# Column totals of an attention kernel moved into the idle PSUM bank of the attention's outputs

## The chip, the cores and the metric

The kernel runs on one core of a Trainium2 chip. The metric is device time in microseconds of one execution. A core has TensorE (PE, with weight loads shown apart as PEld), VectorE (DVE), ScalarE (ACT), GpSimd (POOL) and SyncE (SP, which here issues nearly all DMAs). Matmuls write to PSUM; this kernel cuts PSUM into eight banks of 512 fp32 columns by 128 partitions. A matmul that begins a new use of a bank must wait until the engines that read the bank's last content are done.

## The reference, cut to what matters

One layer of a streaming encoder: 2048 prompt rows and 8 streams of 16 rows with 512 cached keys. Rows are normed, modulated and projected; two attentions run side by side; their outputs are gated, projected, merged and projected again.

```python
qa, ka, va, za, qb, kb, vb, zb, ga, gb = project_inputs(h, w_in[l], pos_p)
oa = diff_attention(qa, ka, va, qpos, kpos, lam)          # A: softmax(q1 k1) - lam softmax(q2 k2), 4 heads
ob = stick_breaking_attention(qb, kb, vb, qpos, kpos)     # B: sigmoids and a running product, 8 heads
ya = (rms_norm(oa, subln_g) * (1 - lam_init) * silu(za)) @ w_branch_a
yb = (ob * silu(zb)) @ w_branch_b
x = x + gate * ((sigmoid(ga) * ya + sigmoid(gb) * yb) @ w_out)
```

All is fp32 outside. The kernel multiplies in fp16, with each operand cut into a high and a low half. For that it needs a power of two as scale of each weight piece and cache piece, and it gets one from the sum of squares of the whole piece: ACT sums the squares along each partition, and a matmul with a 128x128 matrix of ones adds the 128 partition sums up and hands the total to all partitions.

## The kernel before, in words

The attention's work is cut into eight units, `u` = 0 to 7: unit 2h is head h of A, unit 2h+1 is two heads of B. Each unit has 17 row tiles of 128 rows: the sample tile first (`NT`), then prompt tiles t = 0 to 15. A step is one tile of one unit:

- `project` (L467): 24 matmuls of 128x512 into a bank of tag "mm"; ACT and DVE cut the result into fp16 halves of q, k and v. In units of B, `gate_piece` (L543) adds 24 more matmuls per tile, which sum up in the bank of tag "t", and ACT (L548) takes them out.
- `transpose_qk` (L561, L565): six transposes into the bank "t", which DVE or ACT copies out (L575, L576).
- `scores`: for each 512 keys two matmuls (L708, L709) and, at the diagonal, a mask (L712), into a bank of tag "s". For A DVE takes the scores out (L602) and a softmax follows. For B ACT writes two sigmoids (L134), DVE scans them (L682), and POOL multiplies (L688).
- `turn`: the weights are cut into halves (L616, L619; for A L318, L323) and a transposing DMA on SP (L626) brings them into a buffer `wt`, of which there are five (8 blocks of 128 keys each).
- `pv`: the weights times the values, block by block: for A three matmuls (L765 to L767), for B two for each of two heads (L769, L770). They sum up in a bank of tag "o" from the tile's first block to its last, 3(t+1) matmuls for A and 4(t+1) for B. ACT (L744, L749) and DVE (L750) then take the tile out. These products are put off by 27 time units of the kernel's own count, some one and a half tiles.

The PSUM banks before: two of "mm", three of "s", one of "t", two of "o", each tag used in turn. The column totals of `total` (L235, two instructions of a 128x1 product in fp32) went to these:

- `bounds` (L368, in `prepare_unit`): the total of the weights of unit u+1, into "t". DVE computes the scale from it (L243) and copies it (L371). Eight times in the run.
- `bounds_g` (L374): the same for the gate weights of a unit of B, into "t". Four times.
- `halve` (L951): the total of a piece of the cached keys, into "s". DVE reads it (L951), and the piece is then cut into halves on POOL and DVE. 32 times, spread over units 1 to 6.

`kernel` opens the tile framework with `schedule_with_timeline_sim=True`: the framework takes the instructions in the order in which the Python code makes them as their priority, and writes each engine's stream in the order in which, by its own model, operands and buffers come free. So the order of the instructions on an engine is not that of the code, and a tag with fewer buffers or another tag for a tile can move many instructions. Buffers of one tag are handed out in the order of the code. On the chip each engine runs its stream strictly in order.

Of the kernel before, what the change touches and what calls it, by code (L numbers as in the profile page):

```python
# [17 lines left out]
F32 = mybir.dt.float32  # L18
# [4 lines left out]
ALU = mybir.AluOpType  # L23
# [5 lines left out]
KT = D // P  # L29
# [95 lines left out]
def layer_kernel(ctx: ExitStack, tc: tile.TileContext, a: dict):  # L125
    nc = tc.nc
    V, S, G, T = nc.vector, nc.scalar, nc.gpsimd, nc.tensor
# [68 lines left out]
    unit = ctx.enter_context(tc.tile_pool(name="unit", bufs=2))  # L196
# [9 lines left out]
    kvp = c01.enter_context(tc.tile_pool(name="kvp", bufs=2))  # L206
    stg = c01.enter_context(tc.tile_pool(name="stg", bufs=2))

    BANKS = {"mm": 2, "s": 3, "t": 1, "o": 2}

    def bank(tag, dt=F32):
        return ps.tile([P, 512 if dt == F32 else 1024], dt, tag=tag, name=f"ps_{tag}", bufs=BANKS[tag])


# [17 lines left out]
    def total(col, n=1, tag="t"):  # L232

        p = bank(tag)
        T.matmul(p[:, 0:n], ones, col, start=True, stop=True)  # L235
        return p[:, 0:n]
# [66 lines left out]
    def add_up(acc, n):  # L303
        if n == 1:
            return acc[:, 0:1]
        col = tiny.tile([P, 1], F32, tag="col", name="col")
        V.tensor_reduce(out=col, in_=acc[:, 0:n], axis=AX.X, op=ALU.add)
        return col
# [26 lines left out]
    def prepare_unit(u, keep=None):  # L335
# [3 lines left out]
        U = dict(h=h, kind=kind, u=u, w=[], wg=[], bufs=[])  # L339
# [3 lines left out]
        gk = 1024 // gw if gw else 0  # L343
# [21 lines left out]
            return [lambda i=i: piece(i) for i in range(len(ks) + 2)]  # L365

        def bounds():
            fsq = total(add_up(U["wacc"], 4))  # L368
            U["sw"] = scales(fsq, unit, "sw")
            U["fsq"] = unit.tile([P, 1], F32, tag="fsq", name="fsq")  # L370
            V.tensor_copy(out=U["fsq"], in_=fsq)  # L371

        def bounds_g():
            U["sg"] = scales(total(add_up(U["gacc"], KT // gk)), unit, "sg")  # L374

        def split_to(name, k):

# [428 lines left out]
    def cache_column(name, h):  # L806
        return "ab".index(name[0]) * 4 + h
# [106 lines left out]
    def norms():  # L914
# [32 lines left out]
        def halve():  # L947
            st, name, h, i, acc = squared.pop(0)
            c = tiny.tile([P, 3], I32, tag="csc", name="csc", bufs=2)
            f = cexp[:, cache_column(name, h), i : i + 1]  # L950
            V.tensor_scalar(out=c[:, 0:1].bitcast(F32), in0=total(acc, 1, "s"), scalar1=2.0 ** -46, scalar2=None, op0=ALU.max)  # L951
            V.tensor_scalar(out=f, in0=c[:, 0:1], scalar1=24, scalar2=None, op0=ALU.logical_shift_right)
            V.tensor_scalar(out=c[:, 1:2], in0=f, scalar1=-1.0, scalar2=204.0, op0=ALU.mult, op1=ALU.add)
            V.tensor_scalar(out=c[:, 2:3], in0=c[:, 1:2], scalar1=23, scalar2=None, op0=ALU.logical_shift_left)
            to = free.pop(0)
            w = P // 2
            x = to.bitcast(F16).rearrange("p (j f n) -> p j f n", f=2, n=w)
            split(x[:, :, 0, :], x[:, :, 1, :], st.rearrange("p (j n) -> p j n", n=w), c[:, 2:3].bitcast(F32), G)
            load(out=keys_d[name, h, i], in_=x.rearrange("p (j c) f d -> p j (c f d)", c=1))
            free.append(st)  # L960
            free.append(to)
# [3 lines left out]
        def stages(k):  # L965
            if k > 1:
                halve()
            if 0 < k <= len(todo):
                square()
            if k < len(todo):  # L970
                fetch(*todo[k])
# [82 lines left out]
    with tc.tile_pool(name="p0", bufs=1) as p0:  # L1054
# [128 lines left out]
        def wide(x):  # L1183
# [24 lines left out]
                        scalar1=sh[:, 0:1], scalar2=None, op0=ALU.mult)  # L1208
# [208 lines left out]
    for n in range(len(steps) + 2):  # L1417
        made, qk, side = [], [], []
        if n < len(steps):
            u, t = steps[n]  # L1420
# [215 lines left out]
```

## Time and profile before

| what | value |
|---|---|
| runs before | 2221.84, 2226.48, 2226.58 us, median 2226.48 |
| the profiled execution | 2225.32 us, of which the span of the instructions is 2223.5 us |
| PE busy | 2061.2 us (93%) |
| DVE, ACT, POOL busy | 1743.8 (78%), 1606.2 (72%), 699.6 us (31%) |
| mean granted TensorE clock | 0.980 |

In the trace the run has three stages: up to some 136 us the modulation and the norms, up to some 1755 us the eight units, then the branch and output projections with the sample's attention. Busy times of PE are modelled from pipelined matmuls. In the lists of waits a row names the instruction that waited, the one that released it, the sum in us, how often, and the longest.

### The profile page before, as it was taken

What the parts mean: (1) busy time and instruction counts of PE and PEld (TensorE: products, weight loads), DVE (VectorE), ACT (ScalarE), POOL (GpSimd) and SP (SyncE); (2) the same over time, 40 slices, a digit from 0 to 9 for tenths busy, and PEclk for the clock granted to TensorE, in tenths of its full rate; (3) what the DMA queues carried; (4) which work ended last, traced back from release to release, by engine and by line L of the source; (5) the groups of instructions that cost most, each with busy time, mean ns of one, the idle gap of its engine ahead of it and who ended that gap; (6) DMA issues with size and microseconds to landing.
All of it is one profiled execution on the core that took longest, in us unless ns stands there. A gap on an engine that the chain in (4) does not pass through costs nothing. (4 is left out here: it accounts for less than half of the span.)

```text
span 2223.5 us, 41495 instructions
## 1 busy us (share of the span) xinstructions
PE 2061.2 (93%) x14608; PEld 1110.4 (50%) x14608; DVE 1743.8 (78%) x3799; ACT 1606.2 (72%) x3212; POOL 699.6 (31%) x608
## 2 busy tenths in 40 slices
PE   5999999999999999999999998989998788899997
PEld 3655555555555455555554554555454444444443
DVE  4667869789887788988778888777789877787864
ACT  3978677789877677978677788876688666666531
POOL 1232014356410443742024355301334412111210
PEclk8999999999999999999999999999999899999999
DMA  9778559899796889979879999985787999999762
GB/s 323 258 241 201 120 139 217 181 227 203 200 252 158 222 201 202 207 205 221 198 195 216 191 224 207 241 181 130 159 170 155 201 280 255 230 254 224 194 166 67
DMA packets 824978, 451.05 MB, mean 203 GB/s; under 512 B 556122, under 2 KB 763274, under 8 KB 824256
## 3 DMA queue, kind: packets, MB, share of 16 engines
q1 hardware_dynamic: 823820, 448.01, 82.7%
q8 instruction: 114, 1.87, 0.3%
q14 instruction: 96, 0.79, 0.1%
q10 hardware_dynamic: 948, 0.39, 0.1%
HBM read 229.87 MB, written 86.02 MB: 142 GB/s over the span
## 5 line engine op out<-in xcount | busy, mean ns | idle before, releaser
L688 POOL TENSOR_TENSOR sc_p<-sc_p,sc_n 128x127 f32<-128x127 f32 (+7 forms) x192 | 313.3, 1635 | 663.1 <-DVE sc_n L682 510.6
L467 PEld LDWEIGHTS <-hs 128*128 128x128 f16 x3120 | 293.3, 99 | 318.5 <-issue 6.4
L467 PE MATMUL ps_mm<-wa,hs 128*128 128x512 f16 x1590 | 391.2, 382 | 5.3 <-DMA hs<-hT_d 5.0
L467 PE MATMUL ps_mm<-wb,hs 128*128 128x512 f16 x1530 | 377.4, 380 | 0.0
L682 DVE TENSOR_TENSOR_SCAN sc_n<-ps_s,sc_n,zero_t 128x512 f32<-128x512 f32 x192 | 245.4, 1278 | 33.3 <-ACT ps_s L134 28.1
L708 PE MATMUL ps_s<-k,qst 128*128 128x512 f16 (+3 forms) x640 | 223.2, 350 | 30.0 <-DVE sc_n L682 22.8
L543 PEld LDWEIGHTS <-hs 128*128 128x128 f16 x1632 | 155.0, 98 | 181.7 <-DVE qst L576 5.1
L543 PE MATMUL ps_t<-wa,hs 128*128 128x512 f16 x1020 | 242.3, 380 | 2.1 <-DVE qst L576 2.0
L619 DVE TENSOR_TENSOR sc_n<-sc_p,sc_n 128x128 f16<-128x128 f32 (+7 forms) x192 | 217.7, 1137 | 32.9 <-ACT sc_n L616 32.3
L134 ACT ACTIVATE sc_p<-ps_s,usc 128x512 f32<-128x512 f32 (+3 forms) x320 | 203.9, 637 | 34.4 <-PE ps_s L709 23.0
L709 PE MATMUL ps_s<-k,qst 128*128 128x512 f16 (+3 forms) x640 | 223.6, 350 | 0.0
L616 ACT CAST sc_n<-sc_p 128x128 f16<-128x128 f32 (+7 forms) x192 | 155.0, 809 | 57.3 <-POOL sc_p L688 55.8
L134 ACT ACTIVATE ps_s<-ps_s,usc 128x512 f32<-128x512 f32 (+3 forms) x320 | 196.3, 613 | 0.0
L543 PE MATMUL ps_t<-wb,hs 128*128 128x512 f16 x612 | 151.7, 383 | 4.8 <-DMA hs<-hT_d 2.1
L769 PE MATMUL ps_o<-v,wt 128*128 128x128 f16 x1088 | 135.2, 224 | 22.1 <-DMA wt<-sc_n 21.9
L1535 PE MATMUL ps_o<-wo,wb 128*128 128x512 f16 x624 | 141.6, 382 | 1.1 <-ACT wb L1309 1.1
L602 DVE TENSOR_SCALAR_CACHE_REDUCE sc_p<-ps_s,usc 128x512 f32<-128x512 f32 (+3 forms) x160 | 106.2, 664 | 35.7 <-PE ps_s L709 20.5
L770 PE MATMUL ps_o<-v,wt 128*128 128x64 f16 x1088 | 127.1, 196 | 0.0
L769 PEld LDWEIGHTS <-wt 128*128 128x128 f16 x1088 | 101.0, 100 | 50.1 <-DMA wt<-sc_n 25.3
L682 DVE TENSOR_TENSOR_SCAN sc_n<-ps_s,zero_t 128x128 f32<-128x128 f32 (+3 forms) x128 | 104.0, 813 | 27.7 <-ACT ps_s L134 27.7
L1501 PEld LDWEIGHTS <-wa 128*128 128x128 f16 x816 | 77.7, 98 | 94.2 <-issue 4.1
L1544 POOL TENSOR_TENSOR x<-m,x 128x512 f32<-128x512 f32 x32 | 45.6, 1427 | 247.1 <-DVE m L1539 138.7
(378 smaller groups left out, 4548.6 us busy)
## 6 DMA issues: line engine op xcount, KB each, us to landing
hs<-hT_d SPq DMA_DIRECT2D x132, 512.0 KB
g_d<-gt SPq DMA_DIRECT2D x68, 256.0 KB
out_dram<-pr SPq DMA_DIRECT2D x204, 64.0 KB
o_d<-o SPq DMA_DIRECT2D x136, 64.0 KB
wa<-g_d SPq DMA_DIRECT2D x17, 512.0 KB
wb<-g_d SPq DMA_DIRECT2D x17, 512.0 KB
hs<-o_d SPq DMA_DIRECT2D x17, 512.0 KB
wide<-in_w_ada_dram SPq DMA_DIRECT2D x8, 1024.0 KB
```

Of the source, the lines that this page charges most:

```text
L134: i = S.activation(**kw)
L467: T.matmul(box["p"], box["h"][:, hi, k, :], U["w"][k][:, wi, :], start=(n == 0), stop=(n == 3 * KT - 1))
L543: x = T.matmul(box["g"][:, 0:gw], box["h"][:, hi, k, :], U["wg"][k // per][:, k % per, wi, :], start=(j == 0), stop=(j == 3 * KT - 1))
L616: x = S.copy(out=hi, in_=src)
L619: V.tensor_tensor(out=lo, in0=src, in1=hi, op=ALU.subtract)
L682: V.tensor_tensor_scan(out=dst[:, lo : lo + n][:, ::-1], data0=src[:, 0:n][:, ::-1], data1=zero_t[:, 0:1].to_broadcast([P, n]), initial=fi ...
L688: G.tensor_tensor(out=p[:, 0:m], in0=p[:, 0:m], in1=n[:, 1 : m + 1], op=ALU.mult)
L708: T.matmul(p[:, 0:n], qst[:, c, :], kk[:, c, 0:n], start=True, stop=False)
L709: T.matmul(p[:, 0:n], qst[:, 2 + c, :], kk[:, c, 0:n], start=False, stop=not diag)
L769: T.matmul(po[:, c * P : (c + 1) * P], wt[:, wj, :], vt[:, c, :, :], start=first, stop=False)
L770: T.matmul(po[:, c * P : c * P + 64], wt[:, nb + wj, :], vt[:, c, 0, :], start=False, stop=last)
L1535: T.matmul(po, st["y"][:, yi * 8 + k, :], wo[j * 4 + k // 2][:, wi, k % 2, :], start=(n == 0), stop=(n == 3 * KT - 1))
```

## The change

The two banks of "o" become two tags of one bank each, "o0" and "o1". `bank("o")` takes them in turn, by a counter in the code. `bank("other")` names the bank that the last `bank("o")` did not take: the one that the next tile of attention outputs will get. The totals of `bounds`, `bounds_g` and `halve` go there, from "t" and from "s". In `bounds` the copy of the total to SBUF now comes first, and the scale is computed from the copy. The totals of the branch weights, of the cached values and of the modulation stay in "t".

```diff
-    BANKS = {"mm": 2, "s": 3, "t": 1, "o": 2}
+    BANKS = {"mm": 2, "s": 3, "t": 1, "o0": 1, "o1": 1}
+    turn_mm = [0]
 
     def bank(tag, dt=F32):
+        if tag == "o":
+            turn_mm[0] = 1 - turn_mm[0]
+            tag = f"o{turn_mm[0]}"
+        elif tag == "other":
+            tag = f"o{1 - turn_mm[0]}"
         return ps.tile([P, 512 if dt == F32 else 1024], dt, tag=tag, name=f"ps_{tag}", bufs=BANKS[tag])
...
         def bounds():
-            fsq = total(add_up(U["wacc"], 4))
-            U["sw"] = scales(fsq, unit, "sw")
             U["fsq"] = unit.tile([P, 1], F32, tag="fsq", name="fsq")
-            V.tensor_copy(out=U["fsq"], in_=fsq)
+            V.tensor_copy(out=U["fsq"], in_=total(add_up(U["wacc"], 4), 1, "other"))
+            U["sw"] = scales(U["fsq"], unit, "sw")
 
         def bounds_g():
-            U["sg"] = scales(total(add_up(U["gacc"], KT // gk)), unit, "sg")
+            U["sg"] = scales(total(add_up(U["gacc"], KT // gk), 1, "other"), unit, "sg")
...
-            V.tensor_scalar(out=c[:, 0:1].bitcast(F32), in0=total(acc, 1, "s"), scalar1=2.0 ** -46, scalar2=None, op0=ALU.max)
+            V.tensor_scalar(out=c[:, 0:1].bitcast(F32), in0=total(acc, 1, "other"), scalar1=2.0 ** -46, scalar2=None, op0=ALU.max)
```

The engines run the same instructions as before, the same number of them on each; their order differs in many places between the modulation and the end of the units, above all where a unit of B gives way to one of A. Line numbers of the changed kernel are five or six higher from here on: L235 is L241 there, L467 is L472, L769 and L770 are L774 and L775, L765 to L767 are L770 to L772.

The first place is on PE, in unit 3's first prompt tiles, while the last tile of unit 2 (`ps_o_9529`) still takes its products and unit 4's weights get their total. Before, the total is in the bank "t" (`ps_t_9445`):

```order
L766 LDWEIGHTS wt_9121
L766 MATMUL ps_o_9529<-v_6518,wt_9121 128x128
L235 MATMUL ps_t_9445<-col_9443,ones_197 128x1
L708 LDWEIGHTS qst_9287
L708 MATMUL ps_s_9490<-k_9286,qst_9287 128x128
```

In the changed kernel it stands earlier on PE, between the first products of the same tile, in the other bank (`ps_o0`, the tile being in `ps_o1`):

```order
L472 MATMUL ps_mm_9413<-wa1_170,hs1_181 128x512
L770 LDWEIGHTS wt_9121
L770 MATMUL ps_o1_9529<-v_6081,wt_9121 128x128
L241 MATMUL ps_o0_9446<-col_9444,ones_197 128x1
L771 LDWEIGHTS wt_9121
L771 MATMUL ps_o1_9529<-v_6081,wt_9121 128x128
```

What moved is the total, by ten products of the tile, and its bank; the next instruction in that bank is the first product of unit 3's tile 0, some 80 rows on.

The second place is on PE at the end of unit 3 (B), beside the first projections of unit 4's later tiles. `ps_o_12039` is tile 14 of unit 3, `ps_o_12299` its tile 15, and the total (`12020`, in the changed kernel `12021`) belongs to the weights of unit 5. Before, all of tile 14's products are done some 200 rows ahead of the total, which stands among the third quarter of tile 15's:

```order
L769 LDWEIGHTS wt_11973
L769 MATMUL ps_o_12299<-v_10627,wt_11973 128x128
L235 MATMUL ps_t_12020<-col_12018,ones_197 128x1
L770 LDWEIGHTS wt_11973
L770 MATMUL ps_o_12299<-v_10627,wt_11973 128x64
```

In the changed kernel the total is handed the bank `ps_o1` ahead of tile 14, because the code asks for it first. Its matmul stands among projections, and some 45 rows later tile 14's products begin, all sixty in a row, after the first half of tile 15 and in the midst of its third quarter:

```order
L774 LDWEIGHTS wt_11973
L774 MATMUL ps_o0_12299<-v_10279,wt_11973 128x128
L774 LDWEIGHTS wt_11588
L774 MATMUL ps_o1_12039<-v_9935,wt_11588 128x128
L775 LDWEIGHTS wt_11588
L775 MATMUL ps_o1_12039<-v_9935,wt_11588 128x64
```

What moved: tile 14's products from well ahead of tile 15's to behind the total. PE has some 27 projection matmuls of unit 4 ahead of its former order in that stretch. The ends of units 1 and 5 read the same way.

## The prediction

> **What bounds the kernel now.** I read the page's first part, then the busy times by stretch, then the list of PE's waits, then the places where a column total stands.
>
> ```profile
> span 2223.5 us, 41495 instructions
> PE 2061.2 (93%) x14608; PEld 1110.4 (50%) x14608; DVE 1743.8 (78%) x3799; ACT 1606.2 (72%) x3212; POOL 699.6 (31%) x608
> ```
>
> PE is busy for 93% of the span. An average hides stages, so here are stretches of 60 to 100 us of the units (columns: the stretch, its length, then busy us and instructions of PE, PEld, DVE, ACT, POOL, the granted clock, the DMA share, GB/s):
>
> ```profile
> 700.00:800.00 100.00, 92.68 (x637) 50.46 (x636) 76.23 (x163) 76.09 (x166) 36.77 (x35) 1.00 0.81 205
> 900.00:960.00 60.00, 54.80 (x447) 31.23 (x446) 56.55 (x102) 55.48 (x114) 39.52 (x33) 0.97 1.01 206
> 960.00:1020.00 60.00, 59.09 (x397) 32.08 (x398) 50.08 (x134) 48.52 (x112) 26.00 (x29) 0.97 0.73 185
> 1115.00:1215.00 100.00, 92.99 (x641) 50.58 (x639) 77.75 (x165) 76.35 (x168) 37.83 (x35) 1.00 0.85 205
> ```
>
> Two kinds are to be seen. From 700 to 800 and from 1115 to 1215 PE is the busiest by far (93 of 100 us, DVE and ACT 76): a wait of PE there is time lost. From 900 to 960, the end of unit 3, DVE and ACT are fuller than PE (56.6 and 55.5 of 60 against 54.8): there PE's idle time is cheap. Just behind, PE is full again (59.1 of 60). What PE waits for, over the whole run:
>
> ```profile
> PE ps_s L708 <- DVE sc_n L682: 22.8, 25, 2.2
> PE ps_o L769 <- DMA wt<-sc_n: 21.9, 11, 4.2
> PE ps_o L765 <- DMA wt<-sc_n: 18.3, 14, 5.6
> ...
> PE ps_s L235 <- DVE sc_n L682: 6.9, 7, 1.8
> ...
> PE ps_t L235 <- ACT gt L548: 2.7, 2, 1.5
> PE ps_t L561 <- DVE fsq L371: 2.2, 2, 1.1
> ...
> PE ps_s L708 <- DVE csc L951: 1.4, 2, 0.8
> ```
>
> No product of the attention (L765, L769) waits for its bank: only for weights that DMAs bring. The two banks of "o" have slack, and the change spends it. The totals (L235) do wait: for a scan to give a bank of "s" back, and for ACT to empty "t" of gates. And a transpose (L561) and a score (L708) wait because a total sits in their bank unread. In one stretch:
>
> ```profile
> PE ps_s L235 <- DVE sc_n L682: 2.8, 3, 1.8
> PE ps_t L235 <- ACT gt L548: 1.5, 1, 1.5
> PE ps_t L561 <- DVE fsq L371: 1.1, 1, 1.1
> PE ps_s L708 <- DVE csc L951: 0.5, 1, 0.5
> ```
>
> These four are all of PE's listed waits from 720 to 790 us, 5.9 of the 7.3 us that PE idles between 700 and 800. So where PE is the bound, the totals' banks are most of what holds it. At the two longest (start, duration, engine, line, and the idle time before it):
>
> ```profile
> 739.32 0.38 PE L235 MATMUL ps_t<-col,ones 128*128 128x1 f32 x2 [1.54 <-ACT gt L548]
> 757.72 0.38 PE L235 MATMUL ps_s<-cacc,ones 128*128 128x1 f32 x2 [1.80 <-DVE sc_n L682]
> ```
>
> **The change, part by part.** The instructions stay the same in kind and number, so no busy time goes; only waits and orders do.
>
> *Waits that go.* L235 for "s" 6.9, L235 for "t" 2.7, L561 behind a total 2.2, L708 behind a total 1.4: 13.2 us, nearly all in stretches where PE is the bound, so I count them in full, less what comes back: a total in "s" that no longer waits lets PE run on, and the next score may then stand before the same unread bank. The bounds are 0 (projections follow, as behind 757.72) and all 6.9; I take a third, 2.3, since the longest ones have projections or products right behind them. The 32 totals also leave the three banks of "s" to the scores; of the 22.8 us of L708 anything from 0 to a few us may go. I take 0, since these waits are for scans, not for totals.
>
> *Waits that come.* The bank of a total is the one that the next tile's products take. They now wait until DVE has read the total. In unit 2 the slowest read shows how late DVE can be:
>
> ```profile
> 641.59 0.28 PE L235 MATMUL ps_s<-cacc,ones 128*128 128x1 f32 x2
> 647.48 0.15 DVE L951 TENSOR_SCALAR csc<-ps_s 128x1 f32<-128x1 f32 x1
> ```
>
> That is 5.6 us from end to start. In the changed order the next instruction in the total's bank is never fewer than 41 PE rows away, 20 matmuls, most of them projections:
>
> ```profile
> L467 PE MATMUL ps_mm<-wa,hs 128*128 128x512 f16 x1590 | 391.2, 382 | 5.3 <-DMA hs<-hT_d 5.0 <-DVE v L323 0.2
> ```
>
> At 391.2 / 1590 = 0.246 us each that is 4.9 us of cover. Only reads as late as the slowest miss it, by 0.7 us. Two such (units 2 and 4 run alike) make 1.4 us. Ten totals have 41 to 46 rows of cover, so the bounds are 0 and 7 us, if all ten were read so late; with the cover gone it would be 5.6 each. I stay near the low end, as the 5.6 is the slowest of the reads.
>
> *The copy in `bounds`* now runs ahead of the scale. One copy is 0.14 us, eight times 1.1 us at most; PE needs the scale's results a unit later, so I count 0:
>
> ```profile
> L371 DVE COPY fsq<-ps_t x8: 141/144/148, 51.1 to 1372.5; 128x1 f32<-128x1 f32 x8
> ```
>
> *The ends of units 1, 3 and 5.* Here the order shows the one large move: tile 14's sixty products now stand behind the total of a later unit's weights, since that was handed the bank first. In the run before, at the end of unit 3:
>
> ```profile
> 945.50 0.35 ACT L749 ACTIVATE ob<-ps_o,usc 128x128 f32<-128x128 f32 x1
> ...
> 955.15 0.14 DVE L307 TENSOR_REDUCE col<-wacc 128x1 f32<-128x4 f32 x1
> ```
> ```profile
> 955.69 0.22 PE L769 MATMUL ps_o<-v,wt 128*128 128x128 f16 x1
> ...
> 956.03 0.22 PE L769 MATMUL ps_o<-v,wt 128*128 128x128 f16 x1
> 956.09 0.33 PE L235 MATMUL ps_t<-col,ones 128*128 128x1 f32 x2
> ...
> 960.91 0.23 PE L769 MATMUL ps_o<-v,wt 128*128 128x128 f16 x1 [4.18 <-DMA wt<-sc_n]
> ```
>
> Tile 14 was taken out at 945.5, and the total's operand (L307) was there at 955.2. So the products are held back some 10 us, with four of the five `wt` buffers full of their weights, and SP's transposes for tile 15 queue for the fifth, in front of the loads behind them. How much work is held? Four pairs of products start within 956.03 - 955.69 = 0.34 us, 0.085 a pair, so thirty pairs are 2.6 us. For: 27 projection matmuls (27 x 0.246 = 6.6 us) stand in their place, and the held products can fill the 4.18 us that PE waits at 960.91 for tile 15's last weights. Against: they leave a stretch where PE has room for one where it has none, and tile 15's last transpose comes later. Bounds for the three ends together: all of the like waits gone, at most 3 x 4.2 = 12.5 us better; or 3 x 2.6 and as long a new wait each, 3 x (2.6 + 4.2) = 20 us worse. I take 0, between them, as moved work and filled wait are of like size.
>
> The PE's clock hangs on such waits:
>
> ```profile
> 957.00:960.90 3.90, 0.00 (x0) 0.00 (x0) 2.83 (x10) 0.72 (x1) 1.48 (x2) 1.00 0.86 164
> ...
> 961.30:964.70 3.40, 3.40 (x19) 1.58 (x16) 1.88 (x5) 2.14 (x4) 1.80 (x3) 0.50 0.72 149
> ```
>
> After 4.18 us without work the clock was 0.50 for 3.4 us, some 1.7 us of lost work. None of the waits removed (1.8 at most) is that long, so no clock is won with them; a new long wait would cost this on top.
>
> *Sum*, against the profiled execution's own 2225.32 us: -13.2 + 2.3 + 1.4 = -9.5, so 2215.8. The median of the runs shown, 2226.48, is 1.2 above that execution, so I predict **2217 us**.
>
> **The rivals.** (1) *The ends of the units gain as well*: the held products fill the waits for weights, up to 12.5 us. For: the 4.18 above. Against: tile 15's last transpose moves too. Some 2217 - 9 = 2208 us.
>
> (2) *The wait only changes its place*: DVE's read of the total now holds products in place of transposes and scores, and the moved orders cost the rest. For: the bank is handed out in the code's order, and many products stand just 41 to 54 rows behind a total, so that any lag of DVE hits them. Against: the 4.9 us of cover. It gives 2217 + 9.5 = 2226.5 us, no change. [...]
>
> (3) *Slower, by the held products.* One mechanism: at the ends of units 1, 3 and 5 the total comes late, tile 14's products with it, tile 15's last transpose waits for a `wt` buffer, and PE, in order, stands before it. Price for each end: 2.6 of moved work, 4.2 of new wait, 1.7 of halved clock, 8.5 us; three are 25.5, less the 9.5 gained: 2226.5 + 16 = 2242.5 us. It decides from the point where more than one end pays in full: one is 2217 + 8.5 = 2226, two are 2234. For: it is the only place where many instructions moved, and it comes three times. Against: PE has more projections ahead there.
>
> That the change does not do what it says I leave out: the order shows the totals in "o0" and "o1".
>
> **How the numbers follow.** The forecast, 2212 to 2221.5, has 0.42; rival 1 (2204 to 2212) 0.10; rival 2 (2222 to 2230) 0.18; rival 3 (2230 to 2246) 0.30. A measurement of this kernel tells about 0.2% (4.5 us) from no change, so faster means below 2222 and slower above 2231: faster 0.52, same 0.18, slower 0.30. Above 2238 lies half of rival 3, 0.15, and below 2206 a quarter of rival 1, 0.03: 2206 to 2238 holds some 0.8.
>
> **What will show it.** Right: no row of PE's waits with a total (L241) released by a scan or by ACT's gates; no transpose behind the copy; PE's idle time from 700 to 800 and 1115 to 1215 down by some 5 us each; no product waiting for DVE's read (L956, L375) beyond 2 us in all. For the ends: the waits of products for `wt` (40.2 us before in all, L765 and L769) neither up nor down by more than 10. Wrong: if these grow by 15 or more, or the clock falls to 0.5 near 550, 960 and 1375, rival 3 holds; if a row of products released by DVE's read has 8 us or more, rival 2.

## The result, and the profile after

The changed kernel takes 2245.9 us (median of 6 runs, 2243.32 to 2254.88) against 2226.53 us (6 runs) before: ratio 1.0101, 95% interval 1.0084 to 1.0118. It is some 20 us slower, where 9.5 us faster was forecast, and it lies above the range of 2206 to 2238. Its profiled execution took 2244.62 us, with a span of 2242.8.

The page of the changed kernel, first part:

```profile
span 2242.8 us, 41410 instructions
PE 2073.8 (92%) x14608; PEld 1112.8 (50%) x14608; DVE 1756.8 (78%) x3799; ACT 1602.6 (71%) x3212; POOL 699.1 (31%) x608
```

The number of instructions on each of the five engines is as before. PE idles 2242.8 - 2073.8 = 169.0 us (before 162.3), and the same matmuls are busy 12.6 us longer. A matmul's busy time was longer where the granted clock was lower (one of 128x512 took 0.38 us at 768.00, at a clock of 1.00, and 0.59 us at 770.86, at 0.50). The mean granted clock is 0.976 here and 0.973 to 0.977 in the six runs, against 0.980 in the profiled execution of before. Two more executions of before's order (e12 and e16 below) had 0.976 and 0.980 with 158.8 and 161.5 us idle, so a single profile is uncertain by several us in each of the two. As means, idle time is 169.0 against 160.9, and the clock withheld is (1 - 0.975) x 2243 = 56 us against (1 - 0.979) x 2224 = 47. Some 8 us of idle time and at most some 9 us of clock make most of the 20 (at most, since the 56 and 47 also count clock withheld while PE idled, as in 1.84 of the 3.41 us from 768.57 below).

What PE waited for in the changed kernel, whole run (waiting line, releaser, sum, times, longest):

```profile
PE ps_o L774 <- DMA wt<-sc_n: 32.0, 13, 5.3
PE ps_s L713 <- DVE sc_n L687: 18.8, 19, 2.6
PE ps_o L770 <- DMA wt<-sc_n: 10.2, 9, 2.2
...
PE ps_o L241 <- DVE o L755: 6.3, 4, 2.0
...
PE ps_o L241 <- ACT junk L304: 3.5, 2, 2.9
...
PE ps_o L774 <- DVE fsq L375: 1.9, 2, 0.9
...
PE ps_o L241 <- DVE csc L956: 1.1, 2, 0.7
```

The totals (L241, before L235) no longer wait for scans or for gates. They wait for something else: 6.3 us until DVE has taken the previous tile out of the bank (L755), 3.5 for their own operand, and 1.1 until DVE has read the total ahead of them (L956). That is 10.9 us where 9.6 went. Scores wait for scans 18.8 instead of 22.8, and products for their weights 42.2 instead of 40.2.

Busy times by stretch in the changed kernel, for the stretches that the prediction showed of before:

```profile
700.00:800.00 100.00, 92.86 (x628) 50.22 (x627) 80.02 (x161) 74.77 (x165) 36.09 (x35) 0.97 0.75 194
900.00:960.00 60.00, 54.98 (x386) 29.80 (x386) 51.97 (x91) 55.83 (x115) 40.02 (x33) 0.94 0.93 211
960.00:1020.00 60.00, 56.70 (x452) 32.70 (x450) 57.04 (x158) 51.28 (x119) 27.61 (x28) 1.00 0.74 174
1115.00:1215.00 100.00, 91.82 (x596) 48.97 (x595) 73.94 (x160) 70.21 (x156) 31.21 (x30) 0.97 0.80 195
```

From 700 to 800 and 1115 to 1215 PE idles 7.1 and 8.2 us, where it idled 7.3 and 7.0 before. The clock is 0.97 in place of 1.00, and PE gets fewer matmuls done (628 for 637, 596 for 641). From 960 to 1020, where PE was full behind the end of unit 3, it now idles 3.3 us instead of 0.9.

### The profile page after: what moved, and what is told of

It is laid out like the page before. It is cut to its first block, busy times and chain, and to the rows that moved or that the text cites. A ratio compares the mean times of both kernels' runs of the same rounds, so it can differ in the third digit from the quotient of the medians.

```text
span 2242.8 us, 41410 instructions
## 1 busy us (share of the span) xinstructions
PE 2073.8 (92%) x14608; PEld 1112.8 (50%) x14608; DVE 1756.8 (78%) x3799; ACT 1602.6 (71%) x3212; POOL 699.1 (31%) x608
## 5 line engine op out<-in xcount | busy, mean ns | idle before, releaser
L472 PEld LDWEIGHTS <-hs 128*128 128x128 f16 x3120 | 293.3, 99 | 315.2 <-issue 10.7
L472 PE MATMUL ps_mm<-wa,hs 128*128 128x512 f16 x1590 | 399.2, 383 | 5.3 <-DMA hs<-hT_d 4.3
L472 PE MATMUL ps_mm<-wb,hs 128*128 128x512 f16 x1530 | 383.1, 382 | 0.1
L713 PE MATMUL ps_s<-k,qst 128*128 128x512 f16 (+3 forms) x640 | 222.7, 350 | 30.3 <-DVE sc_n L687 18.8
L624 DVE TENSOR_TENSOR sc_n<-sc_p,sc_n 128x128 f16<-128x128 f32 (+7 forms) x192 | 219.3, 1145 | 35.0 <-ACT sc_n L621 34.8
L774 PE MATMUL ps_o<-v,wt 128*128 128x128 f16 x1088 | 129.4, 224 | 33.9 <-DMA wt<-sc_n 32.0
L513 POOL TENSOR_TENSOR rot<-pr,rope 128x256 f32<-128x256 f32 x68 | 62.6, 920 | 251.5 <-ACT pr L486 188.3
L607 DVE TENSOR_SCALAR_CACHE_REDUCE sc_n<-ps_s,usc 128x512 f32<-128x512 f32 (+3 forms) x160 | 106.1, 663 | 31.7 <-PE ps_s L717 22.0
L774 PEld LDWEIGHTS <-wt 128*128 128x128 f16 x1088 | 100.2, 100 | 56.6 <-DMA wt<-sc_n 36.1
```

The costliest lines, as they stand in the source:

```text
L472: T.matmul(box["p"], box["h"][:, hi, k, :], U["w"][k][:, wi, :], start=(n == 0), stop=(n == 3 * KT - 1))
L607: V.tensor_scalar(out=dst[:, lo : lo + n], in0=p[:, 0:n], scalar1=sc_pos, scalar2=None, op0=ALU.mult, op1=ALU.max, accum_out=job["mx"][:, ...
L624: V.tensor_tensor(out=lo, in0=src, in1=hi, op=ALU.subtract)
L713: T.matmul(p[:, 0:n], qst[:, c, :], kk[:, c, 0:n], start=True, stop=False)
L774: T.matmul(po[:, c * P : (c + 1) * P], wt[:, wj, :], vt[:, c, :, :], start=first, stop=False)
```

## Where new idle time and half clock stand: two places

**Behind the ends of the units of B.** The 60 us that follow the ends of units 1, 3 and 5 were full of projections before. Busy time of PE there, then clock, DMA share and GB/s; first the kernel before, then the changed one:

```profile
560.00:620.00 60.00, 59.83 (x426) 1.00 0.74 194
975.00:1035.00 60.00, 60.00 (x432) 1.00 0.75 194
1395.00:1455.00 60.00, 58.55 (x386) 1.00 0.93 232
```
```profile
560.00:620.00 60.00, 54.77 (x394) 1.00 0.74 205
975.00:1035.00 60.00, 56.05 (x382) 1.00 0.76 187
1395.00:1455.00 60.00, 55.43 (x426) 0.97 0.94 221
```

PE idled 1.6 us in the three together, and now 13.8. That is not yet what the ends cost, since PE's waits ahead of them have changed too. The 4.18 us for weights at 960.91 is gone, but the changed kernel has this wait, where the kernel before has none:

```profile
944.91 0.23 PE L774 MATMUL ps_o<-v,wt 128*128 128x128 f16 x1 [3.44 <-DMA wt<-sc_n]
```

What is won and lost over a whole stretch stands with e10 and e17 below.

**In the first tiles of units 3 and 5.** What PE waited for from 720 to 790 us in the changed kernel:

```profile
PE ps_o L241 <- DVE o L755: 2.0, 1, 2.0
PE ps_s L713 <- DVE sc_n L687: 1.9, 1, 1.9
PE ps_o L774 <- DVE fsq L375: 0.9, 1, 0.9
PE ps_o L241 <- DVE csc L956: 0.7, 1, 0.7
PE ps_t L566 <- ACT gt L553: 0.5, 1, 0.5
```

These are 6.0 us; the four rows of before were 5.9. But the two longest now stand side by side. The timeline of the changed kernel there (start, duration, engine, line, in brackets the idle time ahead of it):

```profile
768.00 0.38 PE L713 MATMUL ps_s<-k,qst 128*128 128x512 f16 x1 [1.86 <-DVE sc_n L687]
...
768.68 1.41 DVE L329 SCALAR_TENSOR_TENSOR wb<-wb,sw,wb 128x512 f16<-128x512 f32 x2 [0.48 <-POOL wb L326]
...
770.01 0.34 DVE L755 SCALAR_TENSOR_TENSOR o<-ps_o,usc,ob 128x128 f32<-128x128 f32 x1
...
770.41 0.59 PE L241 MATMUL ps_o<-cacc,ones 128*128 128x1 f32 x2 [2.03 <-DVE o L755]
```

A score waits 1.86 us for a scan, runs 0.38 us, and then the total waits 2.03 us for its bank, since DVE takes the previous tile out (770.01) only after cutting a weight piece (768.68). The bank was idle in the sense that no tile summed up in it; its last tile had not been read. And the clock, in stretches of 3.41 us across that place (length, busy time and instructions of PE, granted clock, DMA share, GB/s):

```profile
765.16:768.57 3.41, 1.36 (x9) 1.00 0.89 262
768.57:771.98 3.41, 1.57 (x5) 0.50 1.12 276
771.98:775.39 3.41, 3.41 (x14) 0.50 0.36 135
```

The clock falls at 768.57, when the total has waited for 0.19 us. In the 3.41 us before that PE was busy for 1.36 us, and 1.86 of the 2.05 us of idle time there are the score's wait for a scan. The total's wait lies in the next 3.41 us, in which PE was busy for 1.57 us, and the clock stays at half for as long again. So at this place the clock fell when the total had hardly begun to wait; that the total's wait cost the second half of the 6.8 us is possible and not shown. The like stands at 1194.10 to 1196.50 us in unit 5 (waits of 2.56 and 2.03 us), where the clock falls at 1195.24.

Before, the like waits of 1.54 and 1.80 us stood 18 us apart, and the clock stayed at 1.00 (739.32 and 757.72 in the prediction's rows). But at other places the kernel before has such falls too, behind scores that wait for scans (from 490.29, 899.89 and 1312.90 us, 3.41 us each); the first:

```profile
488.39 0.32 PE L708 MATMUL ps_s<-k,qst 128*128 128x384 f16 x1 [1.47 <-DVE sc_n L682]
...
489.96 0.38 PE L708 MATMUL ps_s<-k,qst 128*128 128x512 f16 x1 [0.95 <-DVE sc_n L682]
```
```profile
486.88:490.29 3.41, 1.00 (x9) 1.00 0.97 181
490.29:493.70 3.41, 3.41 (x26) 0.50 0.64 144
```

And in the changed kernel a total's wait alone is followed by 3.41 us of half clock, from 341.91:

```profile
341.22 0.38 PE L241 MATMUL ps_o<-cacc,ones 128*128 128x1 f32 x2 [1.82 <-DVE o L755]
```

## The experiments

Four theories. **A**: the products of tile 14, held behind a later unit's total at the ends of units 1, 3 and 5, cost the time (the prediction's rival 3). **B**: totals and products wait for each other in the bank, all over the units (rival 2, at a price). **C**: any order of the instructions other than that of before costs about 1%, in a weaker form 0 to 1.5%. **D**: the copy that now comes ahead of the scale costs. Ratios are to the kernel before, with the 95% interval; 0.1% is 2.2 us. Each ratio rests on 4 to 12 runs of the kernel and 11 to 24 of before.

**e1: the changed kernel without the three totals that hold tile 14.**

```diff
-            V.tensor_copy(out=U["fsq"], in_=total(add_up(U["wacc"], 4), 1, "other"))
+            V.tensor_copy(out=U["fsq"], in_=total(add_up(U["wacc"], 4), 1, "t" if u in (3, 5, 7) else "other"))
```

> The changed kernel, but the weights' totals of units 3, 5 and 7 go back to the bank "t". By that tile 14 of units 1, 3 and 5 is no longer behind a total: its products stand ahead of tile 15's again, as before the change; nothing else of the change is undone, though many rows move with it. Theory A (the sixty held products at the three ends cost the time, about 6.5 us each): about 2226 us, the stretches 545 to 605, 960 to 1020 and 1375 to 1435 as before the change. Theory B (the totals in the other bank wait for the last tile to be taken out, and products for the read): 2243 or more, with L241's waits of some 11 us still there. Theory C (any other order of these instructions costs about 1%): 2240 to 2250.

Measured: 2234.29 us, ratio 1.0047 (1.0030 to 1.0065). Some 12 of the 20 us are gone; none of A, B or C foretold that. PE idles 3.9 us behind the three ends instead of 13.8, as A has it, but the kernel is still slower than before, and its mean clock is 0.972.

**e2: only the weights' totals moved (the cached pieces' back to "s").**

```diff
-            V.tensor_scalar(out=c[:, 0:1].bitcast(F32), in0=total(acc, 1, "other"), scalar1=2.0 ** -46, scalar2=None, op0=ALU.max)
+            V.tensor_scalar(out=c[:, 0:1].bitcast(F32), in0=total(acc, 1, "s"), scalar1=2.0 ** -46, scalar2=None, op0=ALU.max)
```

> The changed kernel, but the 32 totals of the cached pieces go back to "s"; the weights' totals (12) stay in the other bank. The three ends have tile 14 behind a total, as in the changed kernel. Theory A: still slow, 2240 to 2248, perhaps more since the totals in "s" wait for scans again. Theory B: the cached pieces' totals were most of those that wait, so some two thirds of the loss goes: about 2233. Theory C: 2240 to 2250.

Measured: 2243.59, ratio 1.0088 (1.0071 to 1.0106), as A and C said. Taking 32 of the 44 totals out of the bank gives nearly nothing back: B is not most of it.

**e3: only the cached pieces' totals moved, the weights' back to "t".**

```diff
-            V.tensor_copy(out=U["fsq"], in_=total(add_up(U["wacc"], 4), 1, "other"))
+            V.tensor_copy(out=U["fsq"], in_=total(add_up(U["wacc"], 4)))
...
-            U["sg"] = scales(total(add_up(U["gacc"], KT // gk), 1, "other"), unit, "sg")
+            U["sg"] = scales(total(add_up(U["gacc"], KT // gk)), unit, "sg")
```

> The changed kernel, but the weights' totals go back to "t" and only the 32 totals of the cached pieces use the other bank. No tile is behind another's total at the ends of units 1, 3 and 5. Theory A: as fast as before or better by the waits that go in "s", 2218 to 2227. Theory B: most of the loss stays, about 2239. Theory C: 2240 to 2250.

Measured: 2258.76, ratio 1.0157 (1.0136 to 1.0177), the slowest of all, above what every theory said. Tile 14 is not held in it, so A can't be all.

**e4: the kernel before, with only the copy ahead of the scale.**

```diff
-            fsq = total(add_up(U["wacc"], 4))
-            U["sw"] = scales(fsq, unit, "sw")
             U["fsq"] = unit.tile([P, 1], F32, tag="fsq", name="fsq")
-            V.tensor_copy(out=U["fsq"], in_=fsq)
+            V.tensor_copy(out=U["fsq"], in_=total(add_up(U["wacc"], 4)))
+            U["sw"] = scales(U["fsq"], unit, "sw")
```

> The kernel before, with only the order of two DVE instructions changed in bounds: the copy of the total first, the scale from the copy. Banks and tags are those of before. This alone moves some 3200 of PE's 28300 rows. Theories A and B: 2224 to 2228, no change. Theory C: slower by several us, in proportion to the rows moved (5474 rows in the whole change): about 2237.

Measured: 2240.24, ratio 1.0080 (1.0057 to 1.0103): C, or D, which I formed here. Two places catch the eye in the trace. In its order the weights' totals stand right behind gates in "t", in units 3 and 5:

```profile
738.50 0.59 PE L235 MATMUL ps_t<-col,ones 128*128 128x1 f32 x2 [4.72 <-ACT gt L547]
```
```profile
1153.59 0.59 PE L235 MATMUL ps_t<-col,ones 128*128 128x1 f32 x2 [4.62 <-ACT gt L547]
```

Before, the like wait was 1.54 us at 739.32. The clock is at half for 6.8 us at each of the two. Around them, e4 and then before:

```profile
725.00:800.00 75.00, 67.96 (x472) 37.51 (x470) 57.48 (x119) 53.14 (x114) 32.77 (x28) 0.95 0.87 216
1145.00:1220.00 75.00, 68.18 (x484) 38.24 (x483) 58.49 (x122) 53.45 (x116) 32.65 (x28) 0.95 0.85 207
```
```profile
725.00:800.00 75.00, 68.88 (x470) 36.88 (x469) 58.28 (x122) 53.67 (x116) 31.39 (x28) 1.00 0.87 216
1145.00:1220.00 75.00, 68.33 (x494) 37.36 (x492) 61.44 (x127) 57.09 (x124) 31.88 (x29) 1.00 0.89 214
```

A clock of 0.95 withholds 0.05 x 75 = 3.75 us, and PE idles 0.9 and 0.2 us longer, some 8.6 us in all. But these are made good elsewhere: when the kernel before stood at 1600 us, e4's PE had done as much, within 1 us (the table of lags below). Of the 13.9 us by which e4's profiled span is longer than that of before some 11 come from 1600 to 1700 us, in the last tiles of unit 7; 3.5 of them are idle time from 1610 to 1670, where PE was full before.

**e5, e6, e7: the moved totals with the scale first, as before** (all 44; the 12 of the weights; the 32 of the cached pieces).

```diff
+            fsq = total(add_up(U["wacc"], 4), 1, "other")
+            U["sw"] = scales(fsq, unit, "sw")
             U["fsq"] = unit.tile([P, 1], F32, tag="fsq", name="fsq")
-            V.tensor_copy(out=U["fsq"], in_=total(add_up(U["wacc"], 4), 1, "other"))
-            U["sw"] = scales(U["fsq"], unit, "sw")
+            V.tensor_copy(out=U["fsq"], in_=fsq)
```

> The changed kernel, but in bounds the scale is computed from the total first and the copy comes after it, as before the change: the moved totals alone. Theory D (the copy ahead of the scale costs the time; the first four runs all had it, and with nothing else it cost 16 us): 2220 to 2230. Theory A (the held products at the ends of units 1, 3 and 5, which this kernel has): about 2240 to 2246. Theory C (any order of the instructions but that of before costs about 1%, whatever moved it): 2236 to 2258.

> Scale first as before; only the weights' 12 totals go to the other bank, the 32 of the cached pieces stay in "s". Tile 14 stands behind a total at the three ends. Theory D: 2222 to 2230. Theory A: 2240 to 2248. Theory C: 2236 to 2258.

> Scale first as before; only the 32 totals of the cached pieces go to the other bank, the weights' totals stay in "t". No tile is held at the ends of units 1, 3 and 5; at the ends of units 2 and 4 the first products of one tile stand 12 rows behind those of the next. Theory D: 2218 to 2228. Theory A: 2218 to 2228, since there is nothing held at the ends of units of B. Theory B (totals and products wait for each other in the bank): about 2236. Theory C: 2236 to 2258.

Measured: e5 2244.35, ratio 1.0078 (1.0061 to 1.0095); e6 2248.93, 1.0109 (1.0094 to 1.0125); e7 2236.35, 1.0053 (1.0036 to 1.0070). A and C had e5's median; e6 lies at the upper end of A and inside C. D falls as the cause of the whole: without the copy the change costs as much within the intervals. And the parts don't add up: 1.1% and 0.5% alone, 0.8% together. e7 by itself is where B put it, and A missed it: it holds no tile and costs 12 us. But a sum over totals would add up, and e6 with 12 of them costs more than e5 with all 44: B falls.

**e8: the kernel before, with two DVE instructions of the softmax swapped.**

```diff
-            V.scalar_tensor_tensor(out=r[:, 2:3], in0=sums[:, 0:1], scalar=r[:, 1:2], in1=nlam, op0=ALU.mult, op1=ALU.mult)
             V.tensor_tensor(out=r[:, 0:1], in0=r[:, 0:1], in1=ls[:, 0:1], op=ALU.mult)
+            V.scalar_tensor_tensor(out=r[:, 2:3], in0=sums[:, 0:1], scalar=r[:, 1:2], in1=nlam, op0=ALU.mult, op1=ALU.mult)
```

> The kernel before, with its banks and its copy where they were; only two DVE instructions of the softmax, which don't depend on each other (0.1 us each, L661 and L662), change places. By that 2644 of PE's 28321 rows stand elsewhere. Theories A, B and D: 2224 to 2228, no change. Theory C: slower, 2233 to 2245.

Measured: 2223.68, ratio 0.9992 (0.9980 to 1.0005). The strong form of C falls: 2644 rows of PE moved and nothing is lost.

**e9 to e11: the held products alone, at one end, and the change without them.** The totals of units 3, 5 and 7 alone go to the other bank (e9), that of unit 3 alone (e10), all but these three (e11); the scale is first in each. The edit of e9, on top of the split tags:

```diff
-            fsq = total(add_up(U["wacc"], 4))
+            fsq = total(add_up(U["wacc"], 4), 1, "other" if u in (3, 5, 7) else "t")
```

> The kernel before, with only the weights' totals of units 3, 5 and 7 in the other bank: three of the 44 totals, and those behind which tile 14 of units 1, 3 and 5 comes to stand. Scale first, all else as before. Theory A (the held products at the three ends are most of the loss): all of it is here, 2242 to 2250, with 6 to 10 us lost at each end (545 to 650, 950 to 1050, 1350 to 1450) and nothing in between. Theory B (the loss is spread over the totals that wait for their bank and the products that wait for the reads): 3 of 44 totals, 2226 to 2229. Theory C in its weaker form (moved rows cost, here 3559 of PE's 28321): 2230 to 2238, not at the ends above all.

> The kernel before with only the weights' total of unit 3 in the other bank: tile 14 of unit 1 is held at that unit's end, and the order differs from that of before in that stretch alone (930 rows of PE). Theory A: one end's price, 2232 to 2236, lost between 545 and 650 us. Theory B: 2226. Theory C: 2226 to 2229.

> The changed kernel without those three totals (they are in "t") and with the scale first: 41 totals moved, no tile 14 behind a total. Theory A: the change without its fault, 2217 to 2228. Theory B: 2240 or more. Theory C: 2234 to 2246 (4512 rows of PE moved).

Measured: e9 2238.11, ratio 1.0074 (1.0057 to 1.0090); e10 2231.51, 1.0033 (1.0018 to 1.0047); e11 2235.34, 1.0059 (1.0046 to 1.0072). Three of 44 totals cost 0.74% of 2225, 16 us (13 to 20); one costs 7 us (4 to 10), with an order of PE that differs from 521 to 714 us alone. That is A's place, at a price below A's: e9 lies below A's range and at the upper end of C's weaker one, e10 just below A's. e9's order differs on to 1947 us, so not all of its 16 us need come from the three ends. e10's stretch behind the end of unit 1, then what stands there:

```profile
560.00:620.00 60.00, 55.95 (x408) 1.00 0.79 213
```
```profile
570.34 0.22 PE L771 MATMUL ps_o<-v,wt 128*128 128x128 f16 x1 [1.08 <-ACT o L750]
...
578.48 0.39 PE L714 MATMUL ps_s<-k,qst 128*128 128x512 f16 x1 [1.15 <-ACT qst L582]
...
602.07 0.23 PE L771 MATMUL ps_o<-v,wt 128*128 128x128 f16 x1 [1.62 <-DMA wt<-sc_n]
```

(Line numbers here are one higher than in the changed kernel.) PE idles 4.05 us there, before 0.17; behind the end of unit 3, which e10 leaves as it was, it idles 0.00, as before. The longest of the three waits is for weights; the other two are for ACT, which has yet to take the previous tile out (L750) and to copy the transposed q (L582). PE has done projections earlier, beside the held products; that it waits here for this reason is argued from the order.

Over the whole stretch in which the order differs, the two kernels are nearly alike, e10 first and then the kernel before:

```profile
500.00:700.00 200.00, 190.83 (x1402) 1.00 0.87 210
500.00:700.00 200.00, 192.03 (x1435) 1.00 0.89 208
```

PE idles 9.2 us against 8.0 (9.0 and 6.9 in e12 and e16 below, which have the order of before): some 1.2 us more than their mean. The profiled execution took 2225.39 us, the least of e10's six and no more than before's 2225.32. So the 7 us that the runs show are not in this trace, and the 4 us of idle time behind the end are not their account.

e11 is the surprise for A, and inside C: without the held products the rest still costs 13 us (10 to 16), though it idles less than before, 157.3 us. Its clock is 0.973: (0.979 - 0.973) x 2231 is 13 us withheld. Of that 8 stand behind 1755 us, past the units. In the units 6.8 stand at the two places of units 3 and 5, each a total that waits for the previous tile, and then a transpose; the first of them:

```profile
764.93 0.38 PE L241 MATMUL ps_o<-cacc,ones 128*128 128x1 f32 x2 [2.36 <-DVE o L756]
...
767.64 0.37 PE L567 MATMUL ps_t<-id,k 128*128 128x128 f16 x2 [1.41 <-ACT gt L554]
```

Each is followed by 6.8 us at half clock, 3.4 us lost. The kernels that have all or nearly all totals in the other bank (the changed one, e1, e5, e11, and e18 below) have such a half clock at both places, of 6.8 us each but for one of 3.4, and the three executions of before's order (before, e12, e16) have none at either. But half clock in these stretches, 725 to 800 and 1145 to 1220 us, is not the moved totals' own: e4 has 6.8 us in both, e7 and e13 have 3.4 in both, and so has e17 below, whose order of PE there is that of before.

**e12: the tags split, no total moved.** The edit is the first part of the diff alone.

> The kernel before with the bank tag of the outputs split in two and taken in turn, and no total moved: every engine's order is that of before. All theories: 2224 to 2229, and a trace that shows by how much two executions of one order differ from stretch to stretch (some 5 us at most).

Measured: 2225.99, ratio 1.0007 (0.9996 to 1.0018): the tags as such cost nothing. PE idles 1.1 us behind the three ends.

**e13 to e16: what is left.** The nine weights' totals that hold nothing (e13); the six transposes of a tile written in another order (e14); the copy of the transposed q ahead of that of k (e15); the copy of the total second, behind the first instruction of the scale (e16). The last three have the banks of before. Of e13, e15 and e16:

```diff
-            fsq = total(add_up(U["wacc"], 4))
+            fsq = total(add_up(U["wacc"], 4), 1, "t" if u in (3, 5, 7) else "other")
...
-            U["sg"] = scales(total(add_up(U["gacc"], KT // gk)), unit, "sg")
+            U["sg"] = scales(total(add_up(U["gacc"], KT // gk), 1, "other"), unit, "sg")
```
```diff
-        copy(out=kst, in_=pt[:, 0:256].rearrange("p (c n) -> p c n", c=2))
         copy(out=qst, in_=pt[:, 256:768].rearrange("p (j n) -> p j n", j=4))
+        copy(out=kst, in_=pt[:, 0:256].rearrange("p (c n) -> p c n", c=2))
```
```diff
         V.tensor_scalar(out=q, in0=square, scalar1=2.0 ** -46, scalar2=None, op0=ALU.max)
+        if copy is not None:
+            V.tensor_copy(out=copy, in_=square)
...
-            U["sw"] = scales(fsq, unit, "sw")
             U["fsq"] = unit.tile([P, 1], F32, tag="fsq", name="fsq")
-            V.tensor_copy(out=U["fsq"], in_=fsq)
+            U["sw"] = scales(fsq, unit, "sw", copy=U["fsq"])
```

In e14 the loop over the four transposes of q16 in `transpose_qk` stands ahead of that over the two of k16.

> The kernel before, scale first, with only the nine weights' totals in the other bank behind which no tile 14 stands; those of units 3, 5 and 7 in "t", the cached pieces' in "s". 4173 rows of PE stand elsewhere. Theory B (the waits between totals and products in the bank cost; the cached ones are most of them): 2222 to 2229. Theory C, weaker form (an order other than that of before costs up to 1.5%, by how the rows fall and not by the bank): anywhere from 2222 to 2250. Were the prediction's sum right for these nine: 2222.

> The kernel before, banks and copy as they were; only the six transposes of a tile are written in another order (the four of q ahead of the two of k). 3462 rows of PE stand elsewhere. Theory B: 2224 to 2228. Theory C, weaker form: 2222 to 2250, and e14 and e15 not alike.

> The kernel before, banks and the total's copy as they were; only the copy of the transposed q comes ahead of that of k, on the same engine. 3147 rows of PE stand elsewhere. Theory B: 2224 to 2228. Theory C, weaker form: 2222 to 2250.

> The kernel before with the copy of the total as the second of six instructions in bounds, behind the first of the scale and ahead of its other four: four of the scale's five come as late as in the changed kernel, but PE's, ACT's, POOL's and SP's orders are those of before. Theory D (the copy itself costs, by delaying the scale): 2236 to 2242, as where it came first (2240.2). Theory C: 2224 to 2228, since no row moves.

Measured: e13 2238.9, ratio 1.0062 (1.0044 to 1.0079); e14 2231.41, 1.0028 (1.0015 to 1.0041); e15 2233.44, 1.0035 (1.0017 to 1.0053); e16 2225.52, 0.9993 (0.9981 to 1.0005). e16 settles D: where the earlier copy moves no row of PE, it costs nothing, so e4's loss is the order's, not the copy's. Nine totals (e13), 32 (e7) and 41 (e11) cost the same 0.5 to 0.6%, so the price is not one of so much per total. Four reorderings with no bank changed (e8, e14, e15, e4) cost 0, 0.3, 0.35 and 0.8%: the weaker C holds. The prices of the held tiles, 0.74, 0.33 and 0.23%, lie in that range too, and no run holds a tile without changing the order.

**e17, e18: one end again, and the change on another base.** The total of unit 5 alone (e17, the line of e9 with `u in (5,)`); the change with the scale first and e8's swap (e18).

> The kernel before with only the weights' total of unit 5 in the other bank: tile 14 of unit 3 is held at that unit's end, the order differs from that of before in that stretch alone (930 rows of PE, the same rows as in e10 one pair of units later). Theory A: one end's price as in e10, 7 us: 2231 to 2235. If the price in e10 was an accident of that stretch: 2224 to 2229.

> All 44 totals in the other bank, scale first, and the softmax's two instructions swapped as in e8: the change on another base. Tile 14 is held at the three ends. Theory A: 15 to 22 us over e8, 2238 to 2246. Theory C alone (only the order of before is good, and the change has no price of its own): like e14 and e15, 2224 to 2236.

Measured: e17 2227.95, ratio 1.0023 (1.0010 to 1.0035), 5 us (2 to 8), with a median below A's range and inside the one for an accident; e18 2233.16, 1.0052 (1.0033 to 1.0071). In e17 PE idles 3.59 us behind the end of unit 3 and 0.00 behind that of unit 1:

```profile
560.00:620.00 60.00, 60.00 (x432) 1.00 0.75 195
975.00:1035.00 60.00, 56.41 (x414) 1.00 0.79 204
```

It is the mirror image of e10. At the end itself PE is full from 940 to 960 us, first in e17, then in the kernel before:

```profile
940.00:960.00 20.00, 20.00 (x147) 11.03 (x146) 16.62 (x55) 15.30 (x40) 8.63 (x10) 0.95 0.93 225
```
```profile
940.00:960.00 20.00, 16.73 (x159) 10.13 (x157) 19.16 (x59) 17.39 (x42) 10.18 (x11) 1.00 1.01 210
```

But just ahead of that e17 waits for weights, where the kernel before has no such wait:

```profile
938.65 0.23 PE L775 MATMUL ps_o<-v,wt 128*128 128x128 f16 x1 [3.69 <-DMA wt<-sc_n]
```

So the 4.18 us at 960.91 were moved ahead rather than filled. Over the stretch, e17 and then the kernel before:

```profile
930.00:1130.00 200.00, 186.99 (x1361) 0.98 0.82 199
930.00:1130.00 200.00, 188.26 (x1379) 0.99 0.83 201
```

PE idles 13.0 us against 11.7 (11.5 and 12.6 in e12 and e16), some 1.1 us more than their mean. This execution took 2221.78 us, the least of e17's twelve, and it shows the loss no more than e10's does.

7 and 5 us at two ends leave 4 of e9's 16 for the third and for what else e9's order differs in. e18 says that the change costs some 12 us with e8's swap too (7 to 16; e8 itself stood at 0.9992), less than A's 15 and inside C's range; the holds and both of the clock's places are in its trace, with 12.7 us of idle time behind the three ends.

All kernels but e10 and e17 by the idle time of PE in those three stretches of 60 us, which parts them without overlap:

| tile 14 held at all three ends | idle us | not held | idle us |
|---|---|---|---|
| changed kernel | 13.8 | before, e12, e16 | 1.6, 1.1, 2.0 |
| e2, e5, e6 | 14.3, 14.0, 16.0 | e1, e11, e13 | 3.9, 5.5, 4.8 |
| e9 | 11.2 | e3, e4, e7 | 3.1, 2.7, 1.7 |
| e18 | 12.7 | e8, e14, e15 | 9.3, 3.5, 5.3 |

This idle time tells the held tiles and not the loss: e8 idles 9.3 us there and is as fast as before, and e3, the slowest, idles 3.1.

Where time is lost on balance is seen by the work done. I add up the columns that PE's matmuls have streamed (the last number of a row's shape) and ask how much later each execution reaches the sum that the kernel before had at a given time, in us against the mean of before, e12 and e16:

| time in before, us | 540 | 700 | 900 | 1100 | 1200 | 1420 | 1600 | 1700 | end |
|---|---|---|---|---|---|---|---|---|---|
| changed kernel | -5.4 | -0.6 | 3.8 | 9.7 | 14.4 | 20.4 | 11.2 | 12.0 | 17.9 |
| e9 | -1.9 | -1.6 | 1.6 | 2.1 | 1.5 | 5.6 | 0.8 | 1.1 | 4.9 |
| e10 | -0.9 | -0.4 | 1.9 | -0.7 | -0.3 | -1.7 | -2.5 | -2.0 | -1.3 |
| e17 | -0.9 | -2.4 | -2.3 | -0.5 | 0.5 | 0.7 | 0.0 | -0.1 | -4.9 |
| e11 | -6.1 | -4.2 | -2.4 | 1.2 | 5.3 | 2.6 | 4.5 | 4.3 | 6.5 |
| e4 | -3.9 | -3.3 | 0.3 | -2.7 | -1.7 | 0.8 | 0.7 | 11.4 | 12.5 |

The three executions of one order lie up to 2.8 us from their mean at these points, so differences of 3 us mean little. The changed kernel's PE is 5 us ahead at 540 and 20 behind at 1420. Of these 26 us some 11 are lost from 540 to 700 and from 900 to 1100, around and behind the ends of units 1 and 3, and some 9 from 700 to 900 and from 1100 to 1200, in the stretches of the clock's two places; 9 are won back by 1600. So the loss is spread wider than the two places shown above.

No version was faster than the kernel before by more than its interval.

## Why the prediction was wrong, step by step

- **"The ends of units 1, 3 and 5 ... I take 0"** failed. The bounds, 12.5 us better to 20 worse, held the price: alone the three held tiles cost 16 us (e9), at one end 7 or 5 (e10, e17). I had set the moved work against a filled wait. The wait was moved and not filled: the 4.18 us at 960.91 are gone in the changed kernel, but its products wait 3.44 us for weights at 944.91, and 5.30 at 1374.64 in unit 5 (before 3.26, at 1375.97). What I left out is what stood in the moved work's place behind it: 27 projections done early are 6.6 us of work that the next 60 us no longer have, and PE idles 4 us an end there. Whether that is the price stays open: in the traces of e10 and e17 the idle time of the whole stretch grows by some 1 us, and both are executions that don't show the loss. Nor is the held tile parted from a mere change of order, since e4, e7 and e13 hold none and cost 16, 12 and 14 us.
- **"Waits that go", 13.2 less 2.3 back**, failed in the sum. The rows named did go: no total waits for a scan or for gates, no transpose behind the copy. But 10.9 us of waits of the same totals stand where 9.6 went. I had asked only who waits for the total's read, not what the total waits for: the bank's last tile, which DVE takes out late. So the sum's -9.5 was wrong without the ends as well: e11, which holds no tile, is 13 us slower and not 9.5 faster. That is rival 2's outcome by another mechanism.
- **"Waits that come", 1.4**, was right for the wait that it priced: products waited 1.9 us for DVE's read of a total (L375), and the 41 rows of projections covered the rest.
- **No term for the clock**, on the ground that "none of the waits removed (1.8 at most) is that long". That ground was wrong: shorter waits stand ahead of half clock too, 1.47 and 0.95 us in the kernel before (490.29), and a total's wait of 1.82 us in the changed one (341.91). What the missing term was worth is not clear. The two places in units 3 and 5 withhold 6.8 us in the changed kernel, but over the units as a whole half clock withholds 25.6 us, against 20.5, 29.0 and 22.2 in the three executions of before's order. That the total's new wait brings half clock about was not shown: in the traces the one follows the other, and no run took that wait away alone.
- **"The copy ... I count 0"** was right of the copy (e16), and wrong of its place ahead of the scale on before's order (e4, 16 us by the medians), through the order that comes with it. In the changed kernel it makes no difference that the runs can tell (e5 against the changed kernel).
- **Rival 3** had the result, 2242.5 against 2245.9, and in the ends one of the places, but not the mechanism, so the number is luck in good part: the products' waits for `wt` rose by 2 us, where I asked for 15. Half clock within 20 us of 550, 960 and 1375 is 0, 3.4 and 6.8 us in the changed kernel, and 3.4 each in e12, which has the order of before; so that sign does not tell the two kernels apart. PE's new idle time stands behind the end, not at tile 15's last transpose.
- The order's own price (0 to 0.8% for reorderings that change nothing else) stood nowhere in the sum. It is as large as all terms of it.

Open: the cause of the loss as a whole. The runs show what moving each group of totals costs, and not why. The parts don't add. The three held tiles cost 16 us alone, and taking them out of the change gave 12 back (from the changed kernel to e1) or 4 by the ratios and 9 by the medians (from e5 to e11). What makes e3 the slowest, and e13 cost 14 us, is not settled; both lose in idle time and in clock at several places.

## What to carry to other kernels

A bank that no tile is summing in is free only once its last content has been read (in the changed kernel totals waited 6.3 us for DVE to take the last tile out): ask what the new user waits for, as well as who waits for it. When a change moves work from one stretch to another, price the stretch that loses the work: a stretch that has no wait now may get one when its cover is taken (behind the three ends PE idled 1.6 us, and 13.8 with the change). Add up the whole stretch before idle time in one part of it is called a loss. And where a model writes the order, run one or two reorderings that change nothing else before a gain or a loss of half a per cent is put down to the change.

## What the runs showed of the hardware

Half clock stood behind idle time of PE at the places shown here, but not behind every wait of like length. In the kernel before, waits of 1.47 and 0.95 us at 488.39 and 489.96 were followed by 3.41 us at a clock of 0.50 (from 490.29), and one of 4.18 us at 960.91 by as long (from 961.33); behind waits of 1.54 us at 739.32 and 1.80 us at 757.72 the clock was 1.00 for the next 10 us. In the changed kernel a wait of 1.82 us at 341.22 was followed by 3.41 us at 0.50 (from 341.91), and waits of 1.86 and 2.03 us at 768.00 and 770.41 lie around a fall that lasted 6.8 us (from 768.57). So the length of a single wait did not tell whether half clock follows. What does was not shown: no run changed a wait and nothing else.

In three executions of one order the mean granted clock was 0.980, 0.976 and 0.980, which is 9 us of withheld clock between the extremes: a single profile can't tell a term of that size.
